# Compressing cached pages: two neighbouring blocks from three fp32 products of even and odd blocks

## The chip, the cores and the metric

The kernel runs on one core of a Trainium2 chip. The metric is the device time of one execution in microseconds (us). The engines are TensorE (PE; its weight loads are PEld), VectorE (DVE), ScalarE (ACT), GpSimd (POOL) and SyncE (SP), which issues most DMAs. Each engine carries out its instructions in order and waits for the others by semaphores.

## The reference, cut to what matters

One layer of a decoder serves a prompt group (512 tokens) and a sample group (8 sequences of 8 tokens, each with 1024 cached tokens). The sample group's attention compresses the cached keys and the cached values. Segments of 16 tokens are taken; a compressed block covers two neighbouring segments, n and n+1:

```
R = CMP_BLOCK // CMP_STRIDE            # 32 // 16 = 2
seg = k in n_seg segments of 16 tokens # (B, 64, 16, KVH, 64)
n_c = n_seg - R + 1                    # 63 blocks
h = b1
for r in range(R):
    h = h + einsum('bnskd,sdh->bnkh', seg[:, r:r + n_c] + posr[r], w1r[r])
return gelu(h) @ w2 + b2
```

With a and b for the two halves of w1 and s for the segments, block n is a·s(n) + b·s(n+1). The compressed keys give scores, a softmax, and from it the one block to drop out of the selected ones; then come the attention over selected blocks and over a window, and the sum with compressed values.

## The kernel before, in words

The sample group's attention is one phase of the kernel, between the prompt attention and the output projection. It works on pairs of sequences, pr = 0 to 3. `load_pages` (L625) brings a pair's pages into G, a tile of 128 x 16 x 512 in f32, by 16 DMAs of 256 KB from SyncE. Of a page's 512 columns, 0:128 hold the keys to compress, 128:256 the values to compress, 256:384 and 384:512 the keys and values of the selected blocks. The host lays the pages out so (`lay_out`, the `cmp_` line). Pages of pairs 0 and 1 are issued in the prompt attention, those of pair 2 after it; pair 3 takes the buffer of pair 0, so its pages are issued after pair 0's `values`.

`hidden(pr, st)` (L773) is the first layer of the compression, st 0 for keys and 1 for values: 8 positions j times 2 halves r of w1, each an fp32 product of 128 x 128 weights with 256 columns, accumulated in one PSUM tile `pcs`. The half r = 1 is written one column to the left of r = 0, which is how segment n+1 comes to stand on block n. A gelu follows: ScalarE squares and shifts (L1107, L1108), VectorE works on it (L1109, L1110), ScalarE takes the tanh (L1113), VectorE the last product (L1119). `compress_keys` then makes `pk` (the compressed keys), `compress_values` makes `pv`.

`soft(pr)` makes the scores (`w_a`, `w_b`, `s_`), the softmax over compressed keys, `pgs` (its sum over heads), from it on VectorE `pn`, `imp` and `drop`, and with it the selected scores (L856), their maximum (L859), the exp on ScalarE (L860), and the scaling of P on VectorE and GpSimd. `values(pr)` transposes P (`tp`, L875, L880) and sums the values into `o`. The loop is:

```
compress_keys(0, W[0])
for pr in range(4):
    P = soft(pr, W[0])
    compress_values(pr)
    if prev: values(*prev); load_pages(3, gps[0]) if pr == 1
    if pr < 3: W = load_window(pr + 1); load_new(pr + 1); compress_keys(pr + 1, W[0])
values(*prev)
```

The program order says what depends on what; the order of the instructions on each engine is set by the framework's scheduler, which simulates a time line, so a change to one function moves instructions of others. Tiles come from pools with a fixed number of buffers: `pcs`, `pk` and `pv` share two PSUM banks, the gelu's tiles have one buffer each.

Of the kernel before, what the change touches and what calls it, by code (L numbers as in the profile page):

```python
# [11 lines left out]
F32 = mybir.dt.float32  # L12
# [3 lines left out]
AF = mybir.ActivationFunctionType  # L16
ALU = mybir.AluOpType
# [66 lines left out]
def body(tc, I, O):  # L84
    nc = tc.nc
    ctx = ExitStack()
    with ctx:
        _body(ctx, tc, nc, I, O)


def _body(ctx, tc, nc, I, O):
    act, dve, pool, pe, sp = nc.scalar, nc.vector, nc.gpsimd, nc.tensor, nc.sync

    def mm(out, lhsT, rhs, start, stop, first_in_bank=True):
        pe.matmul(out, lhsT, rhs, start=start, stop=stop, skip_group_check=not first_in_bank)  # L95
# [96 lines left out]
    b1p = samp.tile([128, 2, 2], F32, name="b1p")  # L192
# [113 lines left out]
    with ExitStack() as c4:  # L306
        wp0 = c4.enter_context(tc.tile_pool(name="wp0", bufs=4, side="right", reuse_waits="tile"))
        n1 = c4.enter_context(tc.tile_pool(name="n1", bufs=2, side="right", reuse_waits="tile"))
        x = []
        us = []  # L310
        for t in range(5):
            x.append(n1.tile([128, D], F32, name="x", tag="x", bufs=5))
            w = D // 2 if t == 0 else D
# [8 lines left out]
        for t in range(5):  # L322
            if t:
                norm_transpose(n1, pst, "tr", x[t][:tsz[t]], t, g1, AH, AL, AST)
            p = psm.tile([128, 512], F32, name="pd", tag="mm")
# [63 lines left out]
    X, pc, gel = [], [], []  # L389
    for st in range(2):  # L390
        x_ = cp.tile([128, 8, 66], F32, name=f"X{st}")
        p = pst.tile([128, 512], F32, name="pkc", tag="tr")
# [43 lines left out]
    with ExitStack() as c4:  # L436
# [14 lines left out]
        for g2 in range(2):  # L451
            p = pst.tile([128, 4, 128], F32, name="pws", tag="tr")
# [12 lines left out]
        for t, p in enumerate(vps):  # L465
            rows = tsz[t]
            if t == 4:
                tmp = halves(p, 512)
                p = ev.tile([64, 512], F32, name="zg", tag="z")
# [6 lines left out]
            r = rstd_of(gw, mv[:, 1:2], 1.0, rows)  # L476
# [7 lines left out]
        p = pst.tile([128, 2, 64], F32, name="pkn", tag="tr")  # L484
# [4 lines left out]
        for g in range(0, 8, 2):  # L489
            p = pst.tile([128, 2, 4, 64], F32, name="psg", tag="tr")  # L490
# [4 lines left out]
        p = pst.tile([64, 8, 64], F32, name="psgs", tag="tr")  # L495
# [42 lines left out]
    for ml in range(2):  # L538
        for half in range(2):
            p = psm.tile([128, 512], F32, name="pq", tag="mm")  # L540
# [55 lines left out]
    with ExitStack() as c4:  # L596
        def lpool(name, bufs, **kw):
            return c4.enter_context(tc.tile_pool(name=name, bufs=bufs, reuse_waits="tile", **kw))
# [24 lines left out]
        G = {}  # L623
# [105 lines left out]
        for i, _ in enumerate(prompt_attention()):  # L729
            if 2 <= i < 18:  # L730
                next(fill, None)
            if i == 18:
# [7 lines left out]
                w1 = sw.tile([128, 2, 16, 128], F32, name="w1")  # L740
# [8 lines left out]
    with cs as c3:  # L749
# [10 lines left out]
        def load_new(pr):  # L760
            VB[pr] = pp.tile([80, 2, 128], F32, name="VB", tag="VB", bufs=2)
            sp.dma_start(VB[pr][64:72], new_w[:, 2 * pr:2 * pr + 2])
            sp.dma_start(VB[pr][72:80], new_s[:, 2 * pr:2 * pr + 2])

        load_new(0)
        s2_ = lpool("ssm", 2)
        ga_ = lpool("agel", 1)
        psaA = lpool("psaA", 2, space=PSUM)
        pss = lpool("pss2", 3, space=PSUM)
        psm = lpool("psm2", 1, space=PSUM)  # L770
# [1 line left out]

        def hidden(pr, st):  # L773

            x = G[pr].rearrange("p g (t j h n) -> p t j h g n", t=4, j=8, h=2)[:, st]
            pc = psaA.tile([128, 512], F32, name="pcs", tag="acc")
            for j in range(8):
                for r in range(2):
                    mm(pc[:, 1 - r:257 - r].rearrange("p (h g n) -> p h g n", h=2, g=16), w1[:, st, r * 8 + j, :], x[:, j],
                       j == 0 and r == 0, j == 7, False)  # L780
            return gelu(nc, ga_, pc[:, 1:257], 256, b1p[:, st, 0:1], b1p[:, st, 1:2], out="sq")

        def compress_keys(pr, KW):
            gel = hidden(pr, 0)
# [313 lines left out]
def gelu(nc, pool_, src, n, bias, hbias, out=None, rows=128, times=None):  # L1098

    sq = pool_.tile([128, n], F32, name="gsq", tag=f"gsq{n}")  # L1100
    xh = pool_.tile([128, n], F32, name="gxh", tag=f"gxh{n}")
    sq, xh = sq[:rows], xh[:rows]
    if bias is None:
        nc.scalar.activation(sq, src, AF.Square)
        nc.scalar.activation(xh, src, AF.Copy, scale=0.5)
    else:
        nc.scalar.activation(sq, src, AF.Square, bias=bias)  # L1107
        nc.scalar.activation(xh, src, AF.Identity, bias=hbias, scale=0.5)  # L1108
    nc.vector.tensor_scalar(sq, sq, 2.0 * 0.044715, 2.0, op0=ALU.mult, op1=ALU.add)  # L1109
    nc.vector.tensor_tensor(sq, sq, xh, op=ALU.mult)  # L1110
    if times is not None:
        nc.gpsimd.tensor_tensor(xh, xh, times, op=ALU.mult)
    nc.scalar.activation(sq, sq, AF.Tanh, scale=GC)  # L1113
    if isinstance(out, str):
        out = sq
    if out is None:
        out = pool_.tile([128, n], F32, name="gout", tag=f"gout{n}", bufs=2)
        out = out[:rows]
    nc.vector.scalar_tensor_tensor(out, sq, 1.0, xh, op0=ALU.add, op1=ALU.mult)  # L1119
    return out  # L1120
# [8 lines left out]
def lay_out(inputs):  # L1129

    a = {name: np.ascontiguousarray(inputs[name]) for name in _INS}
    c = a["cache_kv"][0]
    n = c.shape[0]
    cmp_ = [c[:, :, st].reshape(n, 8, 8, 2, 2, 64).transpose(0, 3, 5, 2, 4, 1) for st in range(2)]
    parts = cmp_ + [c[:, :, 2].transpose(0, 2, 3, 1), c[:, :, 3]]
    a["cache_kv"] = np.concatenate([x.reshape(n * 128, 128) for x in parts], 1)
    w = a["state_win_kv"][0, :, :, 0].reshape(8, 128, 4, 128)
    a["win_kt"] = np.ascontiguousarray(w.transpose(0, 3, 2, 1)).reshape(8, 128, 512)
    return a
# [16 lines left out]
```

## Time and profile before

| | us |
|---|---|
| median of 3 runs | 833.27 (833.26 to 834.88) |
| the profiled execution | 831.24 |
| its span (first to last instruction) | 829.0 |
| TensorE busy | 793.0 (96%) |
| VectorE, ScalarE, GpSimd busy | 444.6, 347.2, 175.0 |
| mean granted TensorE clock | 0.991 |

The profile is of one execution. In its timeline a row stands for one or several alike instructions of an engine: start, time, engine, line, operation, output<-inputs by the program's names, and in brackets the idle time before and who released it. An fp32 product is two instructions on TensorE. Busy times of products are modelled from their starts and overlap a little.

### The profile page before, as it was taken

The page shows a single profiled execution, that of the slowest core. Times are in us where ns is not written, and L with a number is a line of the kernel's source. Part 1 is how long each engine was busy: PE and PEld are TensorE (multiplying, and loading weights), DVE is VectorE, ACT ScalarE, POOL GpSimd, SP SyncE. Part 2 cuts the span into 40 slices and gives each one's busy share as a digit, 9 for nine tenths or more (in the row PEclk, how much of TensorE's full clock was granted, in tenths as well). Part 3 has the DMA queues.
Part 4 walks back from the last instruction along what each step waited for, and adds up shares of the span by engine and source line. Part 5 has one row for each costly group of instructions (what it writes and reads, how often), then busy time and mean ns, then how long its engine had stood idle before and what let it go on. Part 6 is the DMA issues. An engine that isn't in the chain of part 4 may idle for free.

```text
span 829.0 us, 13177 instructions
## 1 busy us (share of the span) xinstructions
PE 793.0 (96%) x4855; PEld 687.2 (83%) x4855; DVE 444.6 (54%) x972; ACT 347.2 (42%) x856; POOL 175.0 (21%) x219
## 2 busy tenths in 40 slices
PE   5999999999999999799999999999999999999996
PEld 4788978878776777578888998989989899898985
DVE  4553978899864423474746245163452634435325
ACT  5444467888753232451734242242322323232213
POOL 2001844454210011140212010111111111111112
PEclk9999999999999999999999999999999999999998
DMA  8561420100698167193334132141320413302003
GB/s 265 169 194 35 127 62 14 39 2 1 235 334 271 43 213 226 30 284 118 119 111 141 64 99 63 44 153 51 102 88 15 154 51 102 102 16 99 1 1 114
DMA packets 54178, 90.20 MB, mean 109 GB/s; under 512 B 7618, under 2 KB 18850, under 8 KB 53986
## 3 DMA queue, kind: packets, MB, share of 16 engines
q1 hardware_dynamic: 53858, 89.30, 34.0%
q8 instruction: 38, 0.62, 0.3%
q14 instruction: 26, 0.21, 0.1%
q0 software_dynamic: 256, 0.07, 0.0%
HBM read 85.08 MB, written 8.39 MB: 113 GB/s over the span
## 4 chain that ended last, share of the span: by engine, by line
PE 85%; DVE 5%; DMA 3%; ACT 3%; issue 1%; SPq 1%; POOL 1%; POOLq 0%; ACTq 0%; DVEq 0%
PE acc L95 52%; PE pd L95 7%; PE pcs L95 6%; PE o L95 4%; PE pu L95 3%; PE s L95 3%; PE tp L685 2%; PE pq L95 2%; DMA raw<-in_w_in 2%; PE pc L95 1%; DVE wu L107 1%; DVE y L1034 1%; DMA G<-in_cache_kv 1%; ACT Hh L106 1%; ACT wu L106 0%
## 5 line engine op out<-in xcount | busy, mean ns | idle before, releaser
L95 PE MATMUL acc<-Hh,wu 128*128 128x288 f32 x1024 | 206.0, 296 | 0.0
L106 ACT ACTIVATE wu<-raw 128x512 fp32r<-128x512 f32 (+1 forms) x184 | 105.9, 614 | 157.8 <-PE acc L95 119.7
L95 PEld LDWEIGHTS acc<-Hh,wu 128*128 128x128 f32 x1024 | 165.3, 189 | 0.6 <-ACT Hh L106 0.2
L95 PE MATMUL acc<-wu,Fh 128*128 128x512 f32 x512 | 155.5, 389 | 0.0
L95 PE MATMUL acc<-Hl,wu 128*128 128x288 f32 x512 | 151.2, 296 | 0.0
L107 DVE TENSOR_TENSOR wu<-raw,wu 128x512 fp32r<-128x512 f32 x160 | 110.2, 730 | 53.5 <-ACT wu L106 53.5
L95 PEld LDWEIGHTS acc<-wu,Fh 128*128 128x128 f32 x512 | 95.7, 188 | 19.5
L95 PE MATMUL acc<-wu,Fl 128*128 128x512 f32 x256 | 97.1, 389 | 0.0
L95 PEld LDWEIGHTS acc<-Hl,wu 128*128 128x128 f32 x512 | 96.4, 188 | 0.3
L1055 DVE TENSOR_TENSOR f<-relu 128x576 f32<-128x576 f32 x32 | 24.2, 756 | 118.8 <-ACT relu L1054 118.8
L958 DVE TENSOR_TENSOR R<-acc,R 128x512 f32<-128x512 f32 x72 | 47.6, 687 | 62.8 <-PE acc L95 62.6
L1054 ACT ACTIVATE relu<-acc 128x288 f32<-128x288 f32 x64 | 26.1, 408 | 117.8 <-PE acc L95 117.8
L964 POOL TENSOR_TENSOR R<-atm,R 64x512 f32<-64x512 f32 x18 | 30.5, 1701 | 155.0 <-DVE atm L963 148.6
L1057 POOL CAST Fst<-Fh 128x64 fp32r<-128x64 f32 x32 | 23.5, 734 | 176.5 <-ACT Fh L106 119.7
L95 PE MATMUL pcs<-G,w 128*128 128x256 f32 x256 | 58.9, 383 | 0.0
L95 PEld LDWEIGHTS acc<-wu,Fl 128*128 128x128 f32 x256 | 48.1, 188 | 10.1
L95 PE MATMUL pd<-wu,AH 128*128 128x512 f32 (+1 forms) x192 | 55.7, 373 | 0.7 <-ACT wu L106 0.5
L95 PEld LDWEIGHTS pcs<-G,w 128*128 128x128 f32 x256 | 47.3, 190 | 9.7 <-issue 3.6
L661 ACT ACTIVATE P<-s,nm 128x32 f32<-128x32 f32 (+4 forms) x88 | 40.2, 463 | 9.9 <-DVE nm L660 9.5
L107 POOL TENSOR_TENSOR wu<-raw,wu 128x512 fp32r<-128x512 f32 (+1 forms) x24 | 30.1, 1271 | 57.7 <-ACT wu L106 53.9
L95 PE MATMUL acc<-wu,Hh 128*128 128x512 f32 x128 | 40.7, 403 | 0.1
L95 PEld LDWEIGHTS pd<-wu,AH 128*128 128x128 f32 x192 | 34.1, 191 | 7.0 <-ACT wu L106 0.9
(318 smaller groups left out, 1336.2 us busy)
## 6 DMA issues: line engine op xcount, KB each, us to landing
raw<-in_w_ff SPq DMA_DIRECT2D x128, 256.0 KB
G<-in_cache_kv SPq DMA_DIRECT2D x64, 256.0 KB
raw<-in_w_in SPq DMA_DIRECT2D x32, 256.0 KB
raw<-in_w_out SPq DMA_DIRECT2D x16, 256.0 KB
out_wins<-in_state_win_kv SPq DMA_DIRECT2D x8, 504.0 KB
KW<-in_win_kt SPq DMA_DIRECT2D x4, 512.0 KB
W<-in_state_win_kv SPq DMA_DIRECT2D x8, 256.0 KB
R<-in_x_prompt SPq DMA_DIRECT2D x4, 512.0 KB
```

Of the source, the lines that this page charges most:

```text
L95: pe.matmul(out, lhsT, rhs, start=start, stop=stop, skip_group_check=not first_in_bank)
L106: act.activation(hi, src, AF.Copy)
L107: eng.tensor_tensor(lo, src, hi.bitcast(F32), op=ALU.subtract)
L661: act.activation(p_[:, c0:c0 + w], src, AF.Exp, bias=nm[:, br, g:g + 1], accum_out=l[:, br, g:g + 1])
L685: pe.transpose(t_[:w, g * 128:(g + 1) * 128], P[g][:, c0:c0 + w], ident)
L958: dve.tensor_tensor(R[t][:, c0:c0 + 512], p, R[t][:, c0:c0 + 512], op=ALU.add)
L964: pool.tensor_tensor(R[4][:, c0:c0 + 512], tm2, R[4][:, c0:c0 + 512], op=ALU.add)
L1034: dve.scalar_tensor_tensor(y[:rows], R[t], r[:rows], gf[:rows], op0=ALU.mult, op1=ALU.mult)
L1054: act.activation(r[:, i * 288:i * 288 + 288], p[:, :288], AF.Relu)
L1055: dve.tensor_tensor(f2, r, r, op=ALU.mult)
L1057: pool.tensor_copy(Fst[:, m, 0:64], Fh[:, m, 512:576].bitcast(F32))
```

## The change

The host now stores each page's segments by even ones (64 columns) and odd ones (64 columns). With e for an even segment and o for the odd one after it, the even block is a·e + b·o and the odd block a·o + b·e', e' being the next even segment. The kernel forms a·(e-o), (a+b)·o and b·(e'-o), three products of 128 columns, and adds the middle one to the other two: the first sum is the even block, the second the odd one. a+b (`w01`) is made once on GpSimd. The differences are made for each pair by VectorE for keys and by GpSimd for values; `dif` has two buffers, and e-o is written over e in G. After the products ScalarE copies the middle part (`ysum`), VectorE adds it twice into `z` in the former order of columns, and the gelu reads `z` in place of PSUM. Lines after `hidden` move by 21: the gelu's L1109, L1110 and L1119 become L1130, L1131 and L1140, the softmax's L856 and L859 become L877 and L880.

```diff
--- before.py
+++ after.py
@@ -762,9 +762,13 @@
             sp.dma_start(VB[pr][64:72], new_w[:, 2 * pr:2 * pr + 2])
             sp.dma_start(VB[pr][72:80], new_s[:, 2 * pr:2 * pr + 2])
 
+        w01 = lpool("wsum", 1).tile([128, 2, 8, 128], F32, name="w01")
+        for st in range(2):
+            pool.tensor_tensor(w01[:, st], w1[:, st, 0:8], w1[:, st, 8:16], op=ALU.add)
         load_new(0)
         s2_ = lpool("ssm", 2)
         ga_ = lpool("agel", 1)
+        gd_ = lpool("gdif", 2)
         psaA = lpool("psaA", 2, space=PSUM)
         pss = lpool("pss2", 3, space=PSUM)
         psm = lpool("psm2", 1, space=PSUM)
@@ -772,13 +776,30 @@
 
         def hidden(pr, st):
 
-            x = G[pr].rearrange("p g (t j h n) -> p t j h g n", t=4, j=8, h=2)[:, st]
+
+
+            eng = pool if st else dve
+            x0, x1 = (G[pr][:, :, st * 128 + e * 64:st * 128 + e * 64 + 64] for e in range(2))
+            v0, v1 = (x.rearrange("p g (a m) -> p g a m", m=4) for x in (x0, x1))
+            d = gd_.tile([128, 16, 64], F32, name="dif", tag="dif")
+            dv = d.rearrange("p g (a m) -> p g a m", m=4)
+            eng.tensor_tensor(dv[:, :, :, 0:3], v0[:, :, :, 1:4], v1[:, :, :, 0:3], op=ALU.subtract)
+            eng.tensor_tensor(dv[:, 0:15, :, 3], v0[:, 1:16, :, 0], v1[:, 0:15, :, 3], op=ALU.subtract)
+            eng.tensor_copy(dv[:, 15, :, 3], v1[:, 15, :, 3])
+            eng.tensor_tensor(x0, x0, x1, op=ALU.subtract)
             pc = psaA.tile([128, 512], F32, name="pcs", tag="acc")
-            for j in range(8):
-                for r in range(2):
-                    mm(pc[:, 1 - r:257 - r].rearrange("p (h g n) -> p h g n", h=2, g=16), w1[:, st, r * 8 + j, :], x[:, j],
-                       j == 0 and r == 0, j == 7, False)
-            return gelu(nc, ga_, pc[:, 1:257], 256, b1p[:, st, 0:1], b1p[:, st, 1:2], out="sq")
+            for i, (w, x) in enumerate(((w1[:, st, 0:8], x0), (w01[:, st], x1), (w1[:, st, 8:16], d))):
+                for j in range(8):
+                    mm(pc[:, i * 128:i * 128 + 128].rearrange("p (g c) -> p g c", g=16), w[:, j], x[:, :, j * 8:j * 8 + 8],
+                       i == 0 and j == 0, i == 2 and j == 7, False)
+            y = ga_.tile([128, 128], F32, name="ysum", tag="ysum")
+            act.activation(y, pc[:, 128:256], AF.Copy)
+            z = ga_.tile([128, 256], F32, name="z", tag="z")
+            zv = z.rearrange("p (h g m e) -> p e g h m", h=2, g=16, m=4)
+            for e in range(2):
+                dve.tensor_tensor(zv[:, e], pc[:, e * 256:e * 256 + 128].rearrange("p (g h m) -> p g h m", g=16, h=2),
+                                  y.rearrange("p (g h m) -> p g h m", g=16, h=2), op=ALU.add)
+            return gelu(nc, ga_, z, 256, b1p[:, st, 0:1], b1p[:, st, 1:2], out="sq")
 
         def compress_keys(pr, KW):
             gel = hidden(pr, 0)
@@ -1131,7 +1152,7 @@
     a = {name: np.ascontiguousarray(inputs[name]) for name in _INS}
     c = a["cache_kv"][0]
     n = c.shape[0]
-    cmp_ = [c[:, :, st].reshape(n, 8, 8, 2, 2, 64).transpose(0, 3, 5, 2, 4, 1) for st in range(2)]
+    cmp_ = [c[:, :, st].reshape(n, 4, 2, 8, 2, 2, 64).transpose(0, 4, 6, 2, 3, 5, 1) for st in range(2)]
     parts = cmp_ + [c[:, :, 2].transpose(0, 2, 3, 1), c[:, :, 3]]
     a["cache_kv"] = np.concatenate([x.reshape(n * 128, 128) for x in parts], 1)
     w = a["state_win_kv"][0, :, :, 0].reshape(8, 128, 4, 128)
```

Where the instructions stand. First TensorE, before, at the end of the prompt attention (`o<-ptl,Vs`, `o<-pth,Vs` and `tp` of L685 are the prompt's; w_2619 is w1):

```order
L95 MATMUL pcs<-G,w_2619 128x256 [waits DMAHW4_49,DMAHW5_49,DMAHW3_49,DMAHW6_49,DMAHW2_49,DMAHW7_49,DMAHW1_49,DMAHW0_49]
L95 MATMUL pcs<-G,w_2619 128x256 x8
L95 MATMUL o<-ptl,Vs 128x512 [waits DVE_49]
L95 MATMUL o<-pth,Vs 128x512 [waits Activation_49]
L685 MATMUL tp<-cst,P 32x128 [waits Pool_49]
L685 MATMUL tp<-cst,P 128x128 [waits PE_49]
L95 MATMUL o<-ptl,Vs 128x512 [waits DVE_49]
L685 MATMUL tp<-cst,P 128x128 x3
L685 MATMUL tp<-cst,P 128x128 [waits PE_49]
L685 MATMUL tp<-cst,P 128x128 x2
L685 MATMUL tp<-cst,P 128x128 [waits Activation_49]
L95 MATMUL pcs<-G,w_2619 128x256 x7
```

and TensorE after the change at the same place (w_3401 is w01):

```order
L685 MATMUL tp<-cst,P 128x128 [waits Activation_49]
L95 MATMUL o<-ptf,Vc 128x512 [waits DVE_49,Activation_49]
L95 MATMUL o<-pth,Vs 128x512
L95 MATMUL o<-ptl,Vs 128x512
L95 MATMUL o<-pth,Vs 128x512 [waits Activation_49]
L95 MATMUL o<-ptl,Vs 128x512 [waits DVE_49]
L95 MATMUL pcs<-G,w_2619 128x128 [waits DMAHW4_49,DMAHW3_49,DMAHW5_49,DMAHW2_49,DMAHW6_49,DMAHW1_49,DMAHW7_49,DMAHW0_49,DVE_49]
L95 MATMUL pcs<-G,w_2619 128x128 x7
L95 MATMUL pcs<-G,w_3401 128x128 [waits Pool_49]
L95 MATMUL pcs<-G,w_3401 128x128 x7
L95 MATMUL pcs<-dif,w_2619 128x128 x8
L95 MATMUL pk_3471<-gsq,w2z 128x128 [waits DVE_49]
```

Nine and seven of the first keys compression's products stood between the prompt's own; now all 24 stand behind the last of these, and the first waits for VectorE. In the fence of after, `pk` follows directly.

Next VectorE, before, around the gelu of pair 2's keys (L1109 to L1119 are that gelu, L821 begins the next softmax):

```order
L103 TENSOR_SCALAR P_3595<-P_3595,r_3638 128x1032
L101 COPY OTs<-to 64x16 [waits PE_49,Activation_49]
L101 COPY OTs<-to 64x16 x3
L876 COPY PTn<-tp_3925 80x128 [waits PE_49]
L1109 TENSOR_SCALAR gsq<-gsq 128x256 [waits Activation_49]
L1110 TENSOR_TENSOR gsq<-gsq,gxh 128x256 [waits DVE_49,Activation_49]
L1119 SCALAR_TENSOR_TENSOR gsq<-gsq,gxh 128x256 [waits Activation_49]
L821 TENSOR_REDUCE nm_3844<-w_a 128x1 [waits PE_49]
L824 TENSOR_SCALAR rc<-l_3845 128x1 [waits Activation_49]
L844 TENSOR_REDUCE nm_3844<-w_a 128x1
```

and after the change (L800 makes z, L786 to L789 are pair 3's differences, L842 begins the softmax):

```order
L819 TENSOR_TENSOR VB<-pv_3751,b2r 64x256 [waits PE_49]
L897 COPY PTn<-tp_4042 80x128 [waits PE_49]
L800 TENSOR_TENSOR z<-pcs,ysum 128x16x2x4 [waits Activation_49]
L800 TENSOR_TENSOR z<-pcs,ysum 128x16x2x4
L786 TENSOR_TENSOR dif<-G 128x256x3 [waits DMAHW4_49,DMAHW5_49,DMAHW3_49,DMAHW6_49,DMAHW2_49,DMAHW7_49,DMAHW1_49,DMAHW0_49]
L787 TENSOR_TENSOR dif<-G 128x240
L788 COPY dif<-G 128x16
L1130 TENSOR_SCALAR gsq<-gsq 128x256 [waits Activation_49]
L789 TENSOR_TENSOR G<-G 128x16x64 [waits DVE_49,Pool_49]
L1131 TENSOR_TENSOR gsq<-gsq,gxh 128x256 [waits DVE_49,Activation_49]
L1140 SCALAR_TENSOR_TENSOR gsq<-gsq,gxh 128x256 [waits Activation_49]
L842 TENSOR_REDUCE nm_3943<-w_a 128x1 [waits PE_49]
```

Pair 3's differences now stand between z and the gelu's steps, with L786 waiting for all eight DMA queues that bring pair 3's pages.

Last VectorE, before, around the gelu of pair 0's values, from its first step to the maximum over the selected scores (L838 to L842 find `drop`, L798 takes `pv`):

```order
L1109 TENSOR_SCALAR gsq<-gsq 128x256 [waits Activation_49]
L836 SCALAR_TENSOR_TENSOR imp<-e_3477,imp 128x14 [waits DVE_49]
L1110 TENSOR_TENSOR gsq<-gsq,gxh 128x256 [waits DVE_49,Activation_49]
L838 TENSOR_REDUCE mn<-imp 128x1 [waits DVE_49]
L839 SCALAR_TENSOR_TENSOR e_3477<-imp,mn,cst 128x14 [waits DVE_49]
L840 TENSOR_REDUCE mn<-e_3477 128x1 [waits DVE_49]
L1119 SCALAR_TENSOR_TENSOR gsq<-gsq,gxh 128x256 [waits Activation_49]
L842 TENSOR_SCALAR drop<-cst,mn 128x16 [waits DVE_49]
L856 TENSOR_TENSOR P_3462<-s__3494,drop 128x512 [waits DVE_49]
L856 TENSOR_TENSOR P_3462<-s__3498,drop 128x512 [waits PE_49]
L798 TENSOR_TENSOR VB<-pv_3537,b2r 64x256 [waits PE_49]
L859 TENSOR_REDUCE nm_3463<-P_3462 128x1 [waits DVE_49]
```

and after the change, from L861, which is L840 of before:

```order
L861 TENSOR_REDUCE mn<-e_3504 128x1 [waits DVE_49]
L863 TENSOR_SCALAR drop<-cst,mn 128x16 [waits DVE_49]
L877 TENSOR_TENSOR P_3489<-s__3521,drop 128x512 [waits DVE_49]
L877 TENSOR_TENSOR P_3489<-s__3525,drop 128x512 [waits PE_49]
L800 TENSOR_TENSOR z<-pcs,ysum 128x16x2x4 [waits Activation_49]
L800 TENSOR_TENSOR z<-pcs,ysum 128x16x2x4
L880 TENSOR_REDUCE nm_3490<-P_3489 128x1 [waits DVE_49]
L1130 TENSOR_SCALAR gsq<-gsq 128x256 [waits Activation_49]
L1131 TENSOR_TENSOR gsq<-gsq,gxh 128x256 [waits DVE_49,Activation_49]
L884 TENSOR_SCALAR r_3532<-l_3491 128x2 [waits Activation_49]
L885 RECIPROCAL r_3532<-r_3532 128x2 [waits DVE_49]
L1140 SCALAR_TENSOR_TENSOR gsq<-gsq,gxh 128x256 [waits Activation_49]
```

The gelu's steps stood between those that find `drop`; now all of them stand behind the selected scores (L877) and their maximum (L880), and the last one behind two of the steps that follow the exp (L884, L885).

## Rows read from the trace of the kernel before

**Rows 1.** The page: busy time of the engines; the chain by line.

```profile
PE 793.0 (96%) x4855; PEld 687.2 (83%) x4855; DVE 444.6 (54%) x972; ACT 347.2 (42%) x856; POOL 175.0 (21%) x219
...
PE acc L95 52%; PE pd L95 7%; PE pcs L95 6%; PE o L95 4%; PE pu L95 3%; PE s L95 3%; PE tp L685 2%; PE pq L95 2%; DMA raw<-in_w_in 2%; PE pc L95 1%; DVE wu L107 1%; DVE y L1034 1%; DMA G<-in_cache_kv 1%; ACT Hh L106 1%; ACT wu L106 0%
```

**Rows 2.** Windows by stretch: PE, PEld, DVE, ACT, POOL busy; PEclk; DMA; GB/s.

```profile
239.70:251.20 11.50, 11.25 (x52) 8.28 (x50) 4.68 (x10) 3.12 (x7) 0.36 (x1) 1.00 1.06 344
251.20:274.30 23.10, 20.98 (x118) 16.02 (x117) 10.17 (x35) 7.50 (x21) 2.28 (x2) 1.00 0.63 209
274.30:299.50 25.20, 24.05 (x170) 18.88 (x170) 10.28 (x38) 7.75 (x25) 2.30 (x2) 1.00 0.48 160
299.50:324.70 25.20, 24.08 (x171) 18.91 (x171) 10.28 (x38) 7.74 (x25) 2.08 (x1) 1.00 0.63 207
324.70:343.50 18.80, 14.98 (x125) 11.53 (x125) 8.94 (x34) 5.55 (x20) 0.77 (x1) 1.00 0.14 40
```

**Rows 3.** Timeline, end of prompt attention: start, us, engine, line, operation.

```profile
239.69 4.05 PE L95 MATMUL pcs<-G,w 128*128 128x256 f32 x18
...
245.25 3.19 PE L95 MATMUL pcs<-G,w 128*128 128x256 f32 x14
...
251.24 0.71 PE L95 MATMUL pk<-gsq,w2z 128*128 128x128 f32 x4
...
252.12 0.85 DVE L704 TENSOR_TENSOR OTp<-o,otmp 64x256 f32<-64x256 f32 x2 [0.94 <-ACT otmp L700]
```

**Rows 4.** Timeline, gelu of pair 2's values and work beside it.

```profile
309.75 0.47 ACT L1107 ACTIVATE gsq<-pcs,b1p 128x256 f32<-128x256 f32 x1 [0.81 <-PE pcs L95]
...
310.38 0.29 DVE L1109 TENSOR_SCALAR gsq<-gsq 128x256 f32<-128x256 f32 x1
...
310.94 1.92 PE L95 MATMUL o<-G,PT 128*64 128x128 f32 x32
...
311.68 0.43 DVE L1119 SCALAR_TENSOR_TENSOR gsq<-gsq,gxh 128x256 f32<-128x256 f32 x1
```

**Rows 5.** Timeline of SyncE, issue of pair 3's pages.

```profile
287.78 9.53 SPq L628 DMA_DIRECT2D G<-in_cache_kv  x16
```

**Rows 6.** Windows of 1 us: DMA share at 303, clock from 342.

```profile
303.00:304.00 1.00, 1.00 (x7) 0.87 (x6) 0.00 (x0) 0.00 (x0) 0.00 (x0) 1.00 0.16 46
342.00:343.00 1.00, 0.00 (x0) 0.00 (x0) 0.90 (x5) 0.00 (x0) 0.27 (x1) 1.00 0.00 0
345.00:346.00 1.00, 1.00 (x8) 0.55 (x6) 0.00 (x0) 0.81 (x2) 0.00 (x0) 0.50 0.00 0
347.00:348.00 1.00, 1.00 (x18) 0.92 (x18) 0.00 (x0) 0.00 (x0) 0.00 (x0) 1.00 0.00 0
```

**Rows 7.** Timeline, weight loads of pk and pcs.

```profile
299.51 0.52 PEld L95 LDWEIGHTS pk<-gsq,w2z 128*128 128x128 f32 x4 [0.28 <-DVE gsq L1119]
...
299.95 4.62 PEld L95 LDWEIGHTS pcs<-G,w 128*128 128x128 f32 x22
```

**Rows 8.** Groups, the last four of 239 to 350: busy, mean ns, idle.

```profile
L107 DVE TENSOR_TENSOR wu<-raw,wu 128x512 fp32r<-128x512 f32 x160 | 110.2, 730 | 53.5 <-ACT wu L106 53.5
...
L95 PEld LDWEIGHTS pcs<-G,w 128*128 128x128 f32 x256 | 47.3, 190 | 9.7 <-issue 3.6
...
L875 PE MATMUL tp<-cst,P 128*80 128x128 f32 x4 | 1.2, 312 | 3.5 <-DVE P L103 3.5
...
L859 DVE TENSOR_REDUCE nm<-P 128x1 f32<-128x1032 f32 x4 | 4.8, 1210 | 0.0
...
L860 ACT ACTIVATE P<-P,nm 128x1032 f32<-128x1032 f32 x4 | 4.6, 1154 | 11.3 <-DVE nm L859 11.2
```

**Rows 9.** Groups on GpSimd over the whole span.

```profile
L107 POOL TENSOR_TENSOR wu<-raw,wu 128x512 fp32r<-128x512 f32 x16 | 21.7, 1370 | 5.3 <-ACT wu L106 5.3
...
L103 POOL TENSOR_SCALAR P<-P,r 128x512 f32<-128x512 f32 x4 | 8.3, 2088 | 67.2 <-DVE r L865 67.2
L671 POOL TENSOR_SCALAR P<-P,r 128x512 f32<-128x512 f32 x4 | 6.3, 1567 | 0.0
```

## Prediction

> **What bounds the kernel now.** I read the page's busy shares first, then its chain, then the busy time by stretch, then the timeline around each place that the change touches. TensorE is busy 793.0 of 829.0 us, and in the chain its compression products (pcs) hold 6% of the span [rows 1]. The change lies between 239.7 and 343.5 us, and I cut that into five stretches at the products pk, which end a keys compression: to pk of pair 0, pair 0 to 1, 1 to 2, 2 to 3, and to the last pair's transposes. TensorE idles 0.25, 2.1, 1.1, 1.1 and 3.8 us in them [rows 2]: a shorter product pays here, and a new wait is paid in full.
>
> Three things show how tight the cover is. The first keys compression has no time of its own: its products fill TensorE while VectorE and ScalarE finish the prompt attention (18 and 14 instructions from 239.69 and 245.25), and pk starts at 251.24, before the last OTp at 252.12 [rows 3]. The gelu between the last pcs product and pv is a ladder of ScalarE and VectorE; it took 2.36 us from the squaring to the end of the last multiply (309.75 to 312.11), and TensorE ran o<-G beside it [rows 4]. And pair 3's pages are issued from 287.78 and drain by about 303.1 (0.16 of the DMA is left in 303 to 304) [rows 5, 6]; their first product in before is far later, so they bind nothing. Last, the granted clock was 1.00 to 343 us, 0.50 in 345:346 after TensorE had stood idle for 3.5 us before the transposes, and 1.00 again at 347: that is the 1.2 GHz level for about 3 us, or 1.5 us lost [rows 6, 8].
>
> **The change, part by part.** *Products.* Now 16 products of 256 columns, two instructions each. 22 instructions took 4.62 us, of which the first weight load is 0.19, so 0.211 each [rows 7]; a compression is 32 x 0.211 = 6.75. After: 24 products of 128 columns, 48 instructions. The nearest row is pk, the same shape: 4 in 0.52, or 0.11 each [rows 7], so 5.2. Eight compressions save 1.6 each, 12.6 in all. If every weight load (190 ns mean [rows 8]) came to stand in line it would be 48 x 0.19 = 9.1 and a loss of 2.4 each; pk ran four of them without that, so I take 5.2.
>
> *Element work.* VectorE took 0.73 us for a two-input operation of 512 columns, 0.43 for 256 [rows 4, 8]: 1.2 ns a column over a fixed 0.12. A keys compression then adds on VectorE a subtract of 768 (1.0), of 240 (0.4), a small copy (0.15), an in-place subtract of 1024 (1.3) and two adds of 128 (0.27 each). Their strided operands stand in no row; 1.21 us for a reduction over 1032 [rows 8] is the lower end for the large ones, twice that the upper. ScalarE adds a copy of 128 columns: under the 0.47 of its 256 [rows 4], I take 0.3. GpSimd gets the same differences for the values and two sums of the weights; it took 1370 ns for 512 columns [rows 9], so about 2.7 for 1024, 5.5 for a set and 5.4 for the two sums. GpSimd has nothing after 240.2 until a P scaling in each pair, so I count its part as hidden: the first set ends near 251, and the values' first product comes after pk of pair 0, 7 us later.
>
> What the sharing of GpSimd and VectorE does is in the rows: its scaling of 512 columns took 2088 ns in the sample phase, where VectorE scales beside it, and 1567 in the prompt [rows 9]. The Trainium skill, "GPSIMD Engine Reference", section "4.1 Engine selection", advises VectorE for elementwise work on two inputs and puts GpSimd at about half its rate; the trace's 1370 against 730 ns agrees. By that rule the values' differences are on the wrong engine, but as an estimate they would still be in time here.
>
> *Stretch 1, to pk of pair 0: 11.55 us before* (239.7 to 251.24). The first product now waits for VectorE's in-place subtract, which stands behind the differences and behind the last OTp. So the fill goes: the prompt's remaining products run alone (3.45 us of work), with two idle times that I estimate from the order: 1.9 until ScalarE has freed o and VectorE has copied ptf, and 3.0 for ScalarE's copy of the last o, two OTp (0.85 [rows 3]) and VectorE's subtracts (1.3 of it); then the products, 5.2; then a gelu with nothing beside it. In that gelu VectorE's order holds pair 1's differences (1.55) ahead of the z adds (0.54) and pair 1's in-place subtract (1.3) ahead of the first gelu step; the ladder from there took 1.73 (310.38 to 312.11 [rows 4]): 5.0. Sum 3.45 + 1.9 + 3.0 + 5.2 + 5.0 = 18.5: +6.9.
>
> *Stretch 2: 23.1 before.* Work: 48 products 10.4; scores, pgs, pv and transposes 6.4. The values' gelu: z stands behind both drop adds (0.7 each by the 730 ns row), nm (1.21) ahead of the gelu's first step, the exp (1.15) ahead of tanh [rows 8]: 1.4 + 0.5 + 1.2 + 1.15 + tanh and last multiply 0.85, and half a microsecond of the drop chain, is 5.6, and TensorE has nothing left to run. The next keys' gelu is again 5.2 after its products, with 1.7 of transposes beside it: 3.5. The idle before pk of pair 0 and that before this pv are as long as the 3.5 us of [rows 8] or longer, so each is followed by 1.5 lost to the clock as in [rows 6]: 3.0. Sum 28.9: +5.8.
>
> *Stretch 3: 25.2 before.* Work 24.05 less 3.2, less 0.5 by which busy time over-counts here: 20.3. The values' gelu has o<-VB and o<-G (1.92 [rows 4]) beside it: 2.9 left of 5.6. Then the new wait: VectorE's difference for pair 3 stands between z and the gelu of pair 2's keys, and it waits for pair 3's pages. Their issue follows pair 0's o<-G. Before it came 13.4 us after pk of pair 1 (274.35 to 287.78 [rows 2, 5]), now 1.6 less after a pk at 287.05, so at 298.9; landing 14 us after it (4.19 MB, from 287.78 to about 302 before, two W loads taken off [rows 5, 6]) is 312.9. The products end at 308.55 (pv at 302.8 takes 0.6, then 5.2), so pk starts at 312.95 + 1.55 + 1.3 + 1.73 less 0.3 of overlap = 317.25; 7.0 idle after 1.7 of transposes. Behind that waiting subtract stand the gelu, then every reduction of the next softmax: TensorE waits for all of them. Sum 30.2: +5.0.
>
> *Stretch 4: 25.2 before.* 20.3 + 1.5 for the clock after the 7 us + 3.1 (the 1.1 of before and two gelus, each longer by ysum and z, about 0.9): 24.9, -0.3. *Stretch 5: 18.85 before.* One compression less 1.6, gelu a little longer: 17.5, -1.35. After that nothing is touched.
>
> Sum: 6.9 + 5.8 + 5.0 - 0.3 - 1.35 = +16. The profiled execution of before was 831.24 (829.0 and 2.24 around it): 847.3. The median shown, 833.27, is 2.0 higher, which gives 849.3; I say 848.
>
> On the clock, the Trainium skill, "TensorE: Matmul & The Clock Gate", "Part 1: The HAM clock gate", has TensorE at half rate until activity releases it; 0.50 at 345 us [rows 6] agrees. By it the sum has 4.5 us of clock; without it, 843.
>
> **Rivals.** *Covered.* If VectorE's additions and the longer gelus lie beside other products, as the gelu of [rows 4] does, only the saving is left: 831.24 - 12.6 = 818.6, or 820.5 against the median. For it: VectorE is little over half busy [rows 1]. Against: idle of stretch 1 and the page wait hang on single chains with nothing behind them in TensorE's order. It decides when new idle is under 12.6; I count about 29. Chance 0.10.
>
> *A draw.* The page wait goes (the pages land before 308.5, if they are released earlier) and the clock does not fall: 16 - 4.4 - 4.5 = +7.1. To come out even, the subtract of stretch 1 must also be early (-3.0) and pair 0's values' gelu as well covered as pair 1's (-2.7): +1.4, or 832.6. Chance of within 0.2% (about what a measurement of this kernel can tell from no change): 0.05, since four things must fall out well together.
>
> *Waits but no half clock* (the forecast's gaps, each too short or broken up): +11.5, 843 to 845. Chance 0.25, on the slower side.
>
> *GpSimd late* (its differences at twice the price, beside VectorE's, as 2088 against 1567 ns hints): a set of 11 us then ends after the values' first product wants it; in pair 0 two sums and a set, 22 us from 240.2, end at 262 and in the other pairs the P scaling stands behind the next set, so transposes wait up to 4 us. 4 x 2 us on the forecast: 856. It decides from about 8 us a set. Chance 0.15.
>
> The forecast itself 0.45: slower in all 0.85. Range 835 to 859: below, no half clock and half of the page wait; above, GpSimd late with strided subtracts at 1.7 us.
>
> **What the profile of the changed kernel would show.** pcs instructions of 128 columns, 384, at 0.11 us start to start. TensorE idle before the first pcs product, released by VectorE's in-place subtract (L789), about 3 us. Idle before pk and pv, released by VectorE's last gelu step. VectorE idle of about 4 us before the subtract on pair 3's pages (L786), released by the DMA of G. The clock at 0.50 behind those gaps. After the last pair, the same length. Wrong would be: pk of pair 0 before 255 (stretch 1), no DMA behind L786 (stretch 3), or a stretch with 0.2 us a product (saving).

## The result, and the profile after

The changed kernel takes 873.04 us (median of 4 runs, 869.83 to 874.82) against 833.26 before: 1.047 times as long, 95% interval 1.044 to 1.049, or 39.8 us. The forecast was 848, with 859 as its upper end: the sign was right, the size was less than half of what came. The profiled execution of after is 869.83, its span 868.1, so 39.1 us longer than the span before.

The page of after: busy time of the engines, and the granted clock in 40 slices (tenths of full speed).

```profile
PE 798.8 (92%) x4983; PEld 699.3 (81%) x4983; DVE 471.8 (54%) x1004; ACT 350.2 (40%) x864; POOL 202.6 (23%) x237
...
PEclk9999999999977688999999999999999999999999
```

TensorE is busy for 798.8 us, 5.8 us more than in [rows 1], although it has a quarter less to multiply in the compressions; the row of the clock shows why: five slices of 21.7 us in which the mean granted clock was 0.6 to 0.8, from 239 to 347 us.

The five stretches again, from one pk to the next, as in [rows 2] (columns: length, then busy PE, PEld, DVE, ACT, POOL, then PEclk, DMA, GB/s).

```profile
240.00:264.80 24.80, 11.83 (x67) 9.32 (x65) 14.36 (x21) 4.04 (x9) 11.53 (x7) 0.76 0.98 334
264.80:298.40 33.60, 23.40 (x150) 20.13 (x150) 15.45 (x41) 7.92 (x22) 7.86 (x6) 0.75 0.06 17
298.40:333.10 34.70, 27.28 (x203) 23.34 (x203) 16.62 (x46) 8.35 (x27) 7.85 (x6) 0.80 0.45 153
333.10:364.20 31.10, 24.65 (x202) 21.57 (x202) 15.27 (x42) 8.46 (x27) 7.67 (x5) 0.86 0.44 151
364.20:382.60 18.40, 13.95 (x144) 11.37 (x145) 9.89 (x36) 5.89 (x21) 1.71 (x1) 1.00 0.00 1
```

They are 24.8, 33.6, 34.7, 31.1 and 18.4 us long, where [rows 2] has 11.5, 23.1, 25.2, 25.2 and 18.8 (the first of after is cut at 240.0, since the prompt ends 0.2 later there). The clock was 1.00 in all five before; it is 0.75 to 0.86 in the first four now.

What TensorE waited for between 239 and 392 us (in total, times, longest):

```profile
PE pk L95 <- DVE gsq L1140: 12.5, 4, 4.8
PE pv L95 <- DVE gsq L1140: 8.9, 2, 6.9
PE pcs L95 <- DVE G L789: 6.4, 1, 6.4
PE o L95 <- DVE PT L101: 6.0, 2, 4.9
```

The wait for VectorE's last gelu step before pk and pv has grown from 1.8 us in all (1.3 before one pv, 0.5 before one pk) to 21.4. Two more are new: for VectorE's in-place subtract before the first product, and for a copy of VectorE's that stood behind the gelu of pair 2's values. To add all up I took the stretch from 239 us to the first output product (acc) in whole windows of 1 us: idle time is 1 less the busy share, and the time lost to the clock is the busy share times 1 less the granted clock.

| kernel | median us | TensorE idle | lost to the half clock |
|---|---|---|---|
| before (to 354) | 833.3 | 11.9 | 1.6 |
| after (to 392) | 873.0 | 44.6 | 19.3 |

Idle time grew by 32.7 and the clock's loss by 17.7; less the 12.6 that the products save, that is 37.8 of the 39.1 us.

Now the places. The end of the prompt attention, which answers to [rows 3] (timeline: start, us, engine, line, operation, idle before and who released it):

```profile
245.04 1.99 POOL L786 TENSOR_TENSOR dif<-G 128x768 f32<-128x768 f32 x1
245.63 2.22 DVE L786 TENSOR_TENSOR dif<-G 128x768 f32<-128x768 f32 x1
...
249.26 2.34 POOL L789 TENSOR_TENSOR G<-G 128x1024 f32<-128x1024 f32 x1
250.12 2.56 DVE L789 TENSOR_TENSOR G<-G 128x1024 f32<-128x1024 f32 x1
...
252.74 5.52 PE L95 MATMUL pcs<-G,w 128*128 128x128 f32 x32 [6.40 <-DVE G L789]
```

Both engines form differences at the same time, and VectorE's take longer than alone: its subtract of 768 columns took 2.22 us here and 0.96 later (at 260.08, with GpSimd idle), the in-place one 2.56 and later 1.22. GpSimd's own two, 1.99 and 2.34, are what they are later on. The first product starts at 252.74.

The gelu of pair 0's values, which answers to [rows 4]:

```profile
277.48 1.99 POOL L786 TENSOR_TENSOR dif<-G 128x768 f32<-128x768 f32 x1 [5.46 <-PE pcs L95]
...
278.79 1.22 DVE L880 TENSOR_REDUCE nm<-P 128x1 f32<-128x1032 f32 x1
...
280.70 2.34 POOL L789 TENSOR_TENSOR G<-G 128x1024 f32<-128x1024 f32 x1
280.78 2.54 DVE L1131 TENSOR_TENSOR gsq<-gsq,gxh 128x256 f32<-128x256 f32 x1
...
284.29 1.11 PE L95 MATMUL pv<-w2z,gsq 128*64 128x64 f32 x8 [6.95 <-DVE gsq L1140]
```

L1131 is VectorE's product of two SBUF tiles, 0.43 us in the mean before. It began within 0.1 us of GpSimd's subtract, took 2.54 and ended 0.28 after it. The maximum L880, which reads one tile, ran its usual 1.22 beside GpSimd's first two subtracts. The Trainium skill, "GPSIMD Engine Reference", section "1. Specifications", says that GpSimd's SBUF interfaces are shared with VectorE, with contention for VectorE instructions in a two-port mode or with two SBUF inputs; for two SBUF inputs these rows agree. GpSimd's set began here because pair 0's products had just let go of one of the two `dif` buffers (released by pcs), so it fell on the gelu behind the same products; no run gives GpSimd more buffers.

The clock behind that wait (windows of 1 us, columns as above), beside [rows 6]:

```profile
279.00:280.00 1.00, 0.00 (x0) 0.00 (x0) 1.00 (x2) 0.81 (x2) 1.00 (x2) 1.00 0.00 0
281.00:282.00 1.00, 0.00 (x0) 0.00 (x0) 1.00 (x1) 0.28 (x2) 1.00 (x1) 0.50 0.00 0
287.00:288.00 1.00, 1.00 (x6) 1.00 (x6) 0.00 (x0) 0.00 (x0) 0.00 (x0) 0.50 0.00 0
291.00:292.00 1.00, 1.00 (x12) 1.00 (x11) 0.00 (x0) 0.00 (x0) 0.00 (x0) 1.00 0.00 0
```

It fell while TensorE idled and was back only at 290.4, after 6.1 us of uninterrupted products at 1.2 GHz; [rows 6] had about 3 us. Such a stretch follows the waits before pk of pairs 0, 1 and 2 and before pv of pairs 0 and 1, and others follow the first wait and the last ones.

And the pages of pair 3, which answer to [rows 5]:

```profile
313.42 9.49 SPq L628 DMA_DIRECT2D G<-in_cache_kv  x16
...
328.90 0.96 DVE L786 TENSOR_TENSOR dif<-G 128x768 f32<-128x768 f32 x1 [0.59 <-DMA W<-in_state_win_kv]
```

Their issue came at 313.42, as everything was later, and VectorE's subtract on them waited 0.59 us, not the 4 us of the forecast (the products that precede it had slipped even further). (The profile names the loads of W, which came last on the same queues.)

### The profile page after: what moved, and what is told of

Its sections match the earlier page's. It is cut to its first block, busy times and chain, and to the rows that moved or that the text cites. A ratio compares the mean times of both kernels' runs of the same rounds, so it can differ in the third digit from the quotient of the medians.

```text
span 868.1 us, 13528 instructions
## 1 busy us (share of the span) xinstructions
PE 798.8 (92%) x4983; PEld 699.3 (81%) x4983; DVE 471.8 (54%) x1004; ACT 350.2 (40%) x864; POOL 202.6 (23%) x237
## 5 line engine op out<-in xcount | busy, mean ns | idle before, releaser
L95 PEld LDWEIGHTS pcs<-G,w 128*128 128x128 f32 x256 | 42.7, 262 | 10.4 <-DVE G L789 6.8
L95 PE MATMUL pcs<-G,w 128*128 128x128 f32 x256 | 44.4, 349 | 6.4 <-DVE G L789 6.4
```

## The experiments

**The differences of the values on VectorE.**

```diff
-            eng = pool if st else dve
+            eng = dve
```

> All differences on VectorE, those of the values too; GpSimd keeps only the two weight sums. Theory A (while GpSimd runs its two-input operations, VectorE's own SBUF-to-SBUF operations stand still: in the changed kernel L1131 took 1.22 us in the mean instead of 0.43): L1131 is back at 0.43 us, the gap before pv of pair 0 falls from 6.95 to under 5 us, and the time falls to 860 to 867, although VectorE gets 4 x 2.9 us more. Rival B (the half clock behind the gaps is the loss, and who makes the differences matters little): 870 to 876.

Measured: 870.46 (865.81 to 872.11), 1.042 times before (1.038 to 1.046). Groups on VectorE, 239 to 394 us (busy, mean ns, idle before), and then TensorE's waits:

```profile
L786 DVE TENSOR_TENSOR dif<-G 128x768 f32<-128x768 f32 x8 | 7.6, 956 | 23.1 <-PE pcs L95 15.9 <-DMA W<-in_state_win_kv 7.1
...
L1131 DVE TENSOR_TENSOR gsq<-gsq,gxh 128x256 f32<-128x256 f32 x8 | 3.4, 421 | 0.5
```

```profile
PE pv L95 <- DVE gsq L1140: 13.7, 4, 7.9
PE pk L95 <- DVE gsq L1140: 11.3, 4, 4.8
```

L1131 is back at 0.42 us, so it was GpSimd that held it up; but the median fell by only 2.6 us, which the spread of the runs does not set apart from none, and the gap before pv of pair 0 did not fall under 5 us, it rose to 7.87. What VectorE no longer waits for, it now works: four more sets of differences, ahead of the same gelus. Idle 43.3, lost to the clock 21.5 (each kernel is summed to its own first output product). In the time of the kernel, who makes the differences matters little, as rival B had it; theory A named a real stall and no gain that is clear.

**No differences at all.** The four operations in `hidden` are left out, and the third product reads the even blocks (`d = x0`).

> No differences are formed: the three products read the pages as they are (the third the even blocks again), with ysum and z as in the change. What is computed is not the reference's compression. Theory A and B agree that the gaps come from the differences: without them the products are free to fill TensorE, so 833 - 12.6 + about 4 for the longer gelus = 822 to 828. Rival C (ysum, z and the order of the schedule open the gaps by themselves): 838 or more, with idle of 4 us or more before pv of pair 0.

Measured: 838.18 (835.43 to 839.83), 1.005 (1.003 to 1.007). The time came out on the rival's side; its sign of 4 us or more before pv of pair 0 did not, with 2.9. Without a single difference the change is still slower than before: idle 23.1 and lost 8.5, so the saving of 12.6 is gone in longer waits. TensorE's waits:

```profile
PE pk L95 <- DVE gsq L1135: 7.5, 4, 3.2
...
PE pv L95 <- DVE gsq L1135: 2.9, 1, 2.9
```

**The element work beside the products of before.** The weight sums and the four operations per set, into tiles that no product reads:

```diff
+            eng = pool if st else dve
...
+            eng.tensor_tensor(d, x0, x1, op=ALU.subtract)
             pc = psaA.tile([128, 512], F32, name="pcs", tag="acc")
```

> The kernel before, with its 16 products of 256 columns, and beside them the change's element work (the weight sums and all four operations of each difference, on VectorE for keys and on GpSimd for values) into tiles that no product reads. Theory A: GpSimd's operations hold up the gelus on VectorE, L1110 rises above 0.8 us in the mean and the time to 838 to 848. Rival B (only products that wait for the differences cost): 833 to 836.

Measured: 852.58 (851.85 to 853.75), 1.022 (1.020 to 1.025): 18 us more than the kernel before beside it, for work whose results no product reads. Theory A's sign did not come: the gelu's product (L1123 there) stayed at 0.42 us in the mean. The groups on VectorE and the waits:

```profile
L785 DVE TENSOR_TENSOR dif<-G 128x768 f32<-128x768 f32 x4 | 5.6, 1390 | 4.3 <-DMA W<-in_state_win_kv 4.1 <-issue 0.2
...
L1123 DVE TENSOR_TENSOR gsq<-gsq,gxh 128x256 f32<-128x256 f32 x8 | 3.4, 424 | 0.4
```

```profile
PE pv L95 <- DVE gsq L1132: 7.4, 1, 7.4
PE pk L95 <- DVE gsq L1132: 5.8, 2, 5.3
```

TensorE waited 7.4 us at one pv and 5.3 at one pk for a gelu that stood behind differences in VectorE's order. But the mean of 1390 ns above, where e1_dve has 956, says that GpSimd took part, and the timeline before that pv (pair 0, at 281.07) shows it:

```profile
271.69 2.70 DVE L785 TENSOR_TENSOR dif<-G 128x768 f32<-128x768 f32 x1 [0.18 <-issue]
...
275.92 3.42 POOL L788 TENSOR_TENSOR dif<-G 128x1024 f32<-128x1024 f32 x1
...
277.16 2.21 DVE L848 TENSOR_TENSOR e<-pn 128x14 f32<-128x14 f32 x1
```

L785 took 2.70 us beside GpSimd's (0.95 alone), L786 1.45 (0.58 alone), and L848, an add of 14 columns that takes 0.18 alone, 2.21. All three have two SBUF inputs and stand ahead of the gelu: 4.7 us of VectorE's delay at the 7.4 us wait. So theory A's mechanism acted here, on other operations than the one it named. At the pk (5.3) GpSimd was idle, and VectorE's order alone made the wait. Idle 25.6, lost 7.2.

**Products of no use in the gaps, first try.**

```diff
+            for k in range((22, 11, 16, 6)[pr] if st == 0 else (30, 8, 20, 0)[pr]):
+                mm(pc[:, 384:512]..., w1[:, st, k % 8], x1[...], False, False, False)
             y = ga_.tile([128, 128], F32, name="ysum", tag="ysum")
```

> The change, with products of no use (128 columns, into the unused quarter of the pcs bank) behind the last product of each compression: 22, 11, 16, 6 for the keys of pairs 0 to 3, 30, 8, 20, 0 for the values, about 0.22 us each at the full clock, so that TensorE is busy in the gaps before pk and pv. Rival B (the half clock costs 20.96 us of busy time between 230 and 400 us, against 3.1 before): the granted clock stays at 1.00 behind these gaps and the time falls by 10 to 17, to 856 to 863. Theory A alone (the stalls are what costs, the clock only goes with them): 870 or more, the added products taking what the clock gives back.

Measured: 885.43 (880.65 to 887.5), 1.063 (1.060 to 1.066). It does not decide between the two theories. At pk of pair 0:

```profile
259.84 5.08 PE L95 MATMUL pcs<-G,w 128*128 128x128 f32 x44
...
264.95 0.28 ACT L799 ACTIVATE ysum<-pcs 128x128 f32<-128x128 f32 x1 [18.60 <-PE pcs L95]
```

The 44 instructions are the 22 products of no use. ScalarE's ysum waited for all products in the bank of pcs, these too, and began at 264.95 instead of some 5 us before. The products lengthened the gap that they were to fill.

**The same in another bank.** 22, 11, 16, 6 products into the pk bank, 30, 8, 20, 0 into the pv bank, each `mm(pk[:, 384:512], w1[:, 0, k % 8], w1[:, 0, 8 + k % 8], True, True)`.

> As e4_warm, with the added products in the banks of pk and pv in place of that of pcs: in e4_warm ScalarE's ysum waited for the last of them, so they lengthened the gaps that they were to fill. Theory B (half clock costs 17.7 us of the change): the clock stays at 1.00 behind most gaps, busy time lost to it falls from 19.3 to under 10, and the time falls to 856 to 863. Rival (what the clock gives back, the added products take, since they also stand ahead of products of use): 868 or more.

Measured: 862.13 (858.77 to 864.12), 1.031 (1.028 to 1.035): 10.9 us faster than the change, with 113 fp32 products more. Windows in its profile:

```profile
262.00:290.00 28.00, 28.00 (x246) 25.48 (x245) 15.10 (x40) 6.62 (x20) 6.37 (x6) 1.00 0.28 99
290.00:332.00 42.00, 41.55 (x387) 37.16 (x386) 21.29 (x54) 10.54 (x32) 11.80 (x8) 1.00 0.38 127
```

From 262 to 332 us the clock is 1.00 throughout, where after it fell five times. Idle fell by 23.6, from 44.6 to 21.0, which is about what the products of no use take (113 x 0.216 = 24.4); lost to the clock fell by 11.5, from 19.3 to 7.8, and the median by 10.9. So the clock's loss is a cost of its own, and it hangs on TensorE's idling, whatever it multiplies.

That the two numbers are so close is in part chance, as the trace by pairs shows. By pk of pair 2 this kernel was 9.9 us ahead of the change (323.16 against 333.07), although its phase began 4.1 us later (see the last experiment). Then pair 2 gave back 6.4 us (37.6 us to the next pk, 31.2 in the change), in a wait for VectorE's differences on pair 3's pages:

```profile
329.31 0.96 DVE L786 TENSOR_TENSOR dif<-G 128x768 f32<-128x768 f32 x1 [8.21 <-DMA W<-in_state_win_kv]
...
338.28 0.69 PE L95 MATMUL pgs<-P,cst 128*128 128x64 f32 x2 [5.67 <-DVE P L852]
```

VectorE idled 8.21 us before them, GpSimd's set ran beside them (VectorE's in-place subtract took 3.31 us), and TensorE waited 5.67 for the softmax behind them. It is the wait for pages that the forecast had put into the change.

**No differences, no ysum and z.** As e2_raw, and the gelu reads `pc[:, 0:256]`.

> As e2_raw (no differences, products on the pages as they are), and without ysum and z too: the gelu reads 256 columns of pcs from PSUM as in the kernel before. What is computed is not the reference's compression. e2_raw took 838.2 where the saving alone gives 820.5. Theory C (ysum and the two z adds, some 0.9 us in each of eight gelus, open the gaps that the clock then doubles): 820 to 826. Rival D (the shorter products leave the gelus without cover whatever stands in them): 832 to 838.

Measured: 831.76 (829.53 to 834.46), 0.998 (0.996 to 0.9998). TensorE's waits there:

```profile
PE pk L95 <- DVE gsq L1128: 3.9, 4, 2.3
PE pv L95 <- DVE gsq L1128: 3.8, 4, 2.4
```

That is just under rival D's range and above theory C's. ysum and z cost 6.4 us (838.2 less 831.8), where theory C wanted 12 or more; the rest is rival D's: with nothing added, products shorter by 12.6 us make the kernel some 2.6 us faster (834.4 beside it), barely clear of the spread. Idle 17.3 and lost 4.9, where before had 11.9 and 1.6. The gelus are as long as before, and less stands beside them.

**Differences a pair ahead.**

```diff
-        gd_ = lpool("gdif", 2)
+        gd_ = lpool("gdif", 4)
+        prep(0, 0); prep(0, 1)
         compress_keys(0, W[0])
         for pr in range(4):
+            if pr < 3: prep(pr + 1, 0); prep(pr + 1, 1)
             P = soft(pr, W[0])
```

(`prep` holds the four operations, all on VectorE; `hidden` begins with the products.)

> All differences on VectorE, written in the program a pair ahead (those of pair pr+1 ahead of the softmax of pair pr) into four buffers in place of two: on VectorE the gelus then stand ahead of the next differences, and the values' gelu of pair 0 between the steps that find drop, as before the change. The same work as e1_dve. Theory E (what costs is where the differences stand in the order, ahead of a gelu for which TensorE waits): 840 to 850, near e2_raw's 838. Rival F (their 23 us on VectorE cost wherever they stand): 862 or more, as e1_dve's 870.

Measured: 863.35 (858.41 to 864.12), 1.034 (1.032 to 1.037). By its number that is rival F, but the timeline at pk of pair 2 shows another reason:

```profile
317.36 0.96 DVE L785 TENSOR_TENSOR dif<-G 128x768 f32<-128x768 f32 x1 [3.94 <-DMA W<-in_state_win_kv]
...
323.52 1.22 PE L95 MATMUL pk<-gsq,w2z 128*128 128x128 f32 x4 [9.05 <-DVE gsq L1148]
```

The scheduler put pair 3's differences ahead of the gelu of pair 2's keys, as in the change. The pages had not landed, VectorE waited 3.94 us, did both sets, and TensorE idled 9.05 us.

**Each set tied behind what must come first.** As e7_early, with tiny writes into `dif` that read the keys' gelu of the pair before (pairs 1 and 2), the maximum of pair 2's selected scores (pair 3), or pair 0's keys (pair 0's values).

> As e7_early, with each set of differences tied by a tiny write (0.15 us) to something that must come first: those of pairs 1 and 2 to the keys' gelu of the pair before, those of pair 3 to the maximum of pair 2's selected scores, and pair 0's values to pair 0's keys. In e7_early TensorE idled 9.1 us before pk of pair 2, behind VectorE's differences on pair 3's pages, which had not landed. Theory E (place in the order): that wait goes, pk of pair 2 comes within 27 us of pk of pair 1, and the time falls to 846 to 853. Rival F (VectorE's amount): 860 or more.

Measured: 850.24 (848.87 to 851.86), 1.020 (1.016 to 1.024), with the same work on VectorE as e1_dve at 870.46. Its waits:

```profile
PE pk L95 <- DVE gsq L1156: 7.5, 4, 3.2
PE pv L95 <- DVE gsq L1156: 4.8, 1, 4.8
PE pcs L95 <- DMA out_wins<-in_state_win_kv: 4.4, 1, 4.4
...
PE pcs L95 <- DVE G L792: 2.9, 1, 2.9
```

pk of pair 2 comes 22.3 us after pk of pair 1. So 20 of the 32 us that the differences cost on VectorE (870.5 to 838.2 by e1_dve and e2_raw) came from where they stood in VectorE's order. The four buffers that this order needs are part of that step; e7_early has them too, and is at 863. What is left sits at the first compression (first product at 249.79; in e2_raw it is at 241.06), at one pv and at the products of pair 3.

**Products of no use in the kernel before.** 14 behind the last pv that read its gelu, 14 behind the last `to` that read ob.

> The kernel before, with 28 fp32 products of no use, 128 columns each (0.22 us), in the two gaps in which its TensorE stands idle: 14 after the last pair's pv, which read its gelu, and 14 after the last transposes, which read ob. Before, the clock stood at 0.50 for about 3 us behind each gap. Theory B (the clock falls because TensorE idles, and a stretch behind a gap costs 1.5 us): the clock stays at 1.00 in 339 to 360 us and the time falls by 2 to 3.2 us, to 0.996 to 0.9975 of before. Rival (the added products delay the transposes or the first output products by as much): 0.999 to 1.002.

Measured: 844.03 (842.11 to 847.9), 1.012 (1.009 to 1.015): slower, a miss. The timeline, and one window from ahead of the added products:

```profile
239.00:240.00 1.00, 1.00 (x6) 0.83 (x4) 0.78 (x2) 0.00 (x0) 0.00 (x0) 0.50 1.05 385
```

```profile
344.76 2.27 PE L95 MATMUL warm<-w,gsq 128*128 128x128 f32 x18
...
347.55 0.31 PE L884 MATMUL tp<-cst,P 128*80 128x128 f32 x1 [0.40 <-DVE P L103]
...
357.19 4.56 PE L95 MATMUL warm<-w,ob 128*128 128x128 f32 x28
...
359.45 1.29 ACT L106 ACTIVATE wu<-raw 128x512 fp32r<-128x512 f32 x2 [2.58 <-DMA raw<-in_w_out]
...
365.47 0.50 PE L95 MATMUL acc<-wu,Hh 128*128 128x512 f32 x1 [3.72 <-ACT wu L106]
```

The first group did its part: the clock stays at 1.00 after the transposes, and from pv of pair 3 to the issue of the output weights' loads it took 10.6 us (341.87 to 352.44), 11.2 before (337.85 to 349.09). But that is 0.7 us, not 1.5.

Behind the second group the first output product came 13.0 us after the loads' issue, where before it came 5.0. The products of no use took 4.56 us of that, about half of it at half clock. Then TensorE waited 3.72 us for ScalarE's splits of the weights (wu): the first began at 359.45, held by a load, 7.0 us after the issue, where before it began at 353.43, 4.3 us after. Two more waits, of 2.80 and 1.70 us, follow. Why the loads and splits came later no run shows; that cause stays open.

In this execution everything from 239 us on also stood 4.0 us later. The window says why: TensorE ran at half clock for some 7 us at the end of the prompt attention, from 233 to 240 us, a loss of 3.4, where the profiled execution of before has 1.00. The profiled executions of e3_elem, e5_raw_noz and e6_warm2 have such a stretch too, between 231 and 241 us. TensorE idles some 1 us in all near 230 us in every kernel here, and the clock fell after it in these four only; why in these, no run shows. Of the sums from 239 us on it makes 0.7 us at most.

## Why the prediction was wrong

*The kind and the place were right.* The first compression lost its cover and pk and pv wait for VectorE. 24 products of 128 columns run at 0.11 us an instruction at the full clock. After the last pair nothing changed: pk of pair 3 is 39.6 us later, the end of the span 39.1.

*The clock term failed*, and it is the larger part of the error. I had put 1.5 us behind three gaps, 4.5 in all, from the one stretch of [rows 6]. The trace of after has eight such stretches from 239 to 392 us: five lost 2.6 to 3.2 us each, with up to 6.3 us of half clock, and three lost 1.5 to 1.9. Together that is 17.7 us more than before, 13.2 more than I had; e6_warm2 took 11.5 of it away by keeping TensorE busy. The Trainium skill, "TensorE: Matmul & The Clock Gate", "Part 1: The HAM clock gate", has it that activity releases the throttle; the trace agrees (0.50 at 287 us, 1.00 at 291). But the one duration in [rows 6] was not a price for every gap, and I left most gaps out.

*The idle term was too small as well.* The sum of +16 holds 24.1 us of new idle time (16 + 12.6 - 4.5); the traces have 32.7. These 8.6 and the 13.2 of the clock are 21.8 of the 23.1 us by which +16 falls short of 39.1.

*GpSimd "hidden" failed.* Its sets were in time, as I had said; but while they ran, VectorE's operations on two SBUF tiles were held up to about their end. I weighed GpSimd's own speed and not this, and read a row such as [rows 9], 2088 against 1567 ns, as a price on GpSimd alone. The first product came 4.7 us later than forecast (252.74 for 248.0), and 3.5 of that lie in VectorE's subtracts: L786 and L789 as shown and L787, 1.46 in place of 0.57. The gelu of pair 0's values left an idle time of 6.95 us where I had 5.6, and that of pair 2's one of 4.86 where I had about 0.9 for a longer gelu. What GpSimd's part costs the kernel is not measured: e1_dve took it away and gained 2.6 us at the median, within the spread, since the same work then stood in VectorE's order.

*The page wait failed.* Of the 7.0 us of TensorE's idle time in stretch 3, 4.4 were for pair 3's pages; VectorE waited 0.59 for them and TensorE 3.71 in all. This term was too large, so it hid a part of what the others lacked. In kernels with less delay the wait is there: VectorE waited 3.94 us for the pages in e7_early and 8.21 in e6_warm2, and TensorE idled 9.05 and 5.67 behind it.

*The saving of 12.6 us* is real on TensorE and is not the kernel's. Taking it off every stretch was sound only with all the new idle time charged beside it. e5_raw_noz shows that 2.6 us of it are left even when nothing is added, because the products were also the cover of the gelus.

By stretches, against the forecast of +6.9, +5.8, +5.0, -0.3 and -1.35: pk of pairs 0 to 3 came 13.6, 24.0, 33.6 and 39.6 us later, so +13.6, +10.4, +9.5 and +6.0, and -0.5 to the end.

In sum, from before: -12.6 for the products, +11.1 for gelus with less cover and the clock behind them (e5_raw_noz at 831.8), +6.4 for ysum and z (e2_raw), +12.1 for differences where they stood best (e9_tied at 850.2), +20.2 for their place in the order (e1_dve at 870.5), +2.6 for half of them on GpSimd (after at 873.0). Each step is a difference of medians, which vary by some 2 us from run to run, so the last is not clear of none; and another order of the steps could share the sum out otherwise. What stays open is how much of the 12.1 and 20.2 is clock: only in the whole kernel was the clock taken out.

None of the versions here that form the differences beats the kernel before. Not tried: differences on GpSimd with more buffers, or tied as in e9_tied.

## What to carry to other kernels

Where products are also what hides a chain on the other engines, shortening them moves the wait, and a long wait on TensorE can be paid a second time at half clock, and for longer than a single stretch elsewhere in the trace suggests (2.6 to 3.2 us here, 1.5 there). Work that prepares operands costs by its place in an in-order queue: the same instructions took 20 us more where they stood ahead of a step that TensorE waited for. Before moving elementwise work to GpSimd, ask which VectorE operations with two SBUF inputs will run at that moment.

## What was not expected of the hardware

VectorE's product of two SBUF tiles took 2.54 us beside GpSimd's subtract of 1024 columns and 0.42 without it; in e3_elem even an add of 14 columns took 2.21 in place of 0.18. A tensor_scalar of one tile also took 0.76 (279.92) in place of 0.29, while a reduction of 1032 columns kept its 1.22. GpSimd itself was faster than estimated: 2.34 us for 1024 columns, where I had 2.7. The half clock lasted 6.1 us in uninterrupted fp32 products (284.3 to 290.4) and 6.3 behind the next pv, and about 3 us in [rows 6]. After the same pause of some 1 us near 230 us it came in some profiled executions and not in others.
